# One step of a hybrid diffusion backbone: the scheduler's machine model is exchanged

## The chip, the cores and the metric

The kernel runs on one core of a Trainium2 chip. What is compared is the device time of one execution in microseconds. A core has five engines that each work through an instruction queue of their own, in the order in which the program holds it: TensorE (PE in the rows; its weight loads are PEld), VectorE (DVE), ScalarE (ACT), GpSimd (POOL) and SyncE (SP). Here SP does nothing but issue DMAs.

## What is computed

One layer on 512 latent and 128 context tokens of width 1024 (640 tokens together), cut to what matters:

```python
h = _rmsnorm(x, p['norm1_g']) * (1.0 + sc1) + sh1        # sc, sh, g from cond @ ada_w
u = h @ p['w_in']                                        # ONE input projection
y_a = _pool_mixer(z_pool, ...)                           # window means
y_b = _fourier_mixer(z_four)                             # 2-D Fourier per group
y_c = rwkv7(r, k, v, w, kk, a)                           # bidirectional, state 64x64
y_d = gla_chunked(q, kg, vg, log_a)                      # bidirectional, gated linear attention
branch = einsum('blic,icd->blid', stack(y_a, y_b, y_c, y_d), p['w_branch'])
gates = sigmoid(m_log)                                   # 4 x 1024 columns of u
out = sum(gates * branch, axis=2) @ p['w_out']
xf = x + g1 * out
h = _rmsnorm(xf, p['norm2_g']) * (1.0 + sc2) + sh2
xf = xf + g2 * (square(relu(h @ p['mlp_w1'])) @ p['mlp_w2'])
y = _rmsnorm(xf, final_g)
```

The outputs are the normalised tokens and the final RWKV and GLA states of the context.

## The kernel before

**Arithmetic.** Large products are made from two halves: an operand is split into a rounded part and a rest (`wh`/`wl`, `xh`/`xl`), and three products are added up in PSUM (`terms`, L363 to L369, for the first half of the kernel; `hidden`, L1356, and L1407 for the MLP). A weight tile comes by DMA into one of three buffers `wr` (`fetch`, L238), is rounded on ScalarE (L246) and its rest is formed on VectorE (L247); two pairs `wh`/`wl` exist.

**Units of work.** `proj(c0)` (L475) makes 128 columns of the input projection for all 640 tokens: 8 k-steps x 3 terms x 2 halves = 48 matmuls of line L368, into one of two PSUM pairs `pm`. There are 51 such tiles; 32 of them are gate columns, made by `gate(i, dt)` (L1187) for mixer i, which ends in a Tanh on ScalarE into one of three buffers `gate`. `branch(i, dt, y)` (L1194) projects a mixer's output with 12 matmuls of L368.

**Stages in the order of the source.** The head (L379 to L472) normalises the tokens and makes the first conditioning columns. Pool and Fourier mixers follow (L522 to L597), then the rest of the conditioning (`ada_rest`, L319: VectorE sums of line L309 over weights `araw`, closed by small matmuls at L315 or L335). The RWKV mixer (L686 to L980) runs twice, for two pairs of heads; each pass builds its triangular matrices (L775), inverts them on VectorE (a loop of 30 dependent steps, L798 to L803) and then takes 8 dependent steps over chunks (L915 to L965: matmuls L921, L935, L944 with VectorE and ScalarE copies between). The GLA mixer (L996 to L1176) has seven levels, each with VectorE and ScalarE work before five matmuls of L1084. The source then lists the merging (L1218 to L1233): for mixers 0 and 1 gate and branch per 128 columns; for mixer 2 the eight gates are made ahead and parked in DRAM (`gscr`, L1224) until the RWKV output is there. Mixer 3 is merged with the output projection (L1250 to L1274). The MLP (L1354 to L1440) is four groups of 8 hidden tiles (L1361, 48 matmuls of 320 columns each) and two halves of the down projection (L1407), the last half apart at L1427.

**What sets the order.** The source is not the order of execution. The framework traces all instructions with their dependencies, and when the `TileContext` closes, its scheduler lays them out: it plays the program on a model of the machine, and each time an engine is free in that model it hands it the instruction of the highest priority that is ready there, and gives out buffers as it goes. Priority follows the order of the source, except in `hi()` and `first()` blocks (L141 to L149), which are raised. So the projections and gates, which depend on nothing but `xh`, `xl` and their weights, are put wherever the model sees TensorE free while RWKV or GLA work isn't ready. The order that results is written into the five queues. The model's durations decide that order and nothing else.

The line that changes is in `kernel()`:

## Time and profile before

| | us |
|---|---|
| median of 3 runs | 1223.72 (1221.15 to 1225.99) |
| the profiled execution, its own time | 1224.66 |
| its span from first to last instruction | 1222.9 |
| TensorE busy / VectorE / ScalarE / GpSimd | 1176.4 / 733.5 / 506.7 / 62.3 |
| mean granted TensorE clock | 0.988 |

Busy time is the union of an engine's instructions. A matmul's end is modelled, so that a busy TensorE is not one at its peak; its true rate is read from the time that a run of equal matmuls takes. In tables of stretches the columns are from:to, the length, then busy us (and instructions) of PE, PEld, DVE, ACT and POOL, the granted clock as a share of full speed, the busy share of the DMA engines and GB/s. "Chain" is the chain of work that ended last, followed back from the last instruction through whatever released each step.

### The profile page before, as it was taken

The numbers are of one execution on the slowest core, as the hardware profiler recorded it, in microseconds if no ns is written. First come the engines' busy times: TensorE is split into PE (matmuls) and PEld (weight loads), VectorE is DVE, ScalarE is ACT, GpSimd is POOL, SyncE is SP. The second block draws the span as 40 slices with busy tenths as digits, with TensorE's granted clock in tenths as the row PEclk, the third lists the DMA queues.
The fourth block names the chain that finished last, engine by engine and source line by source line (L and its number), as shares of the span: only waits on it lengthen the run. The fifth ranks groups of instructions, "written<-read, shape, count | busy, mean of one in ns | idle before, by whom it ended". The sixth has DMA issues, their size and how long they took to land.

```text
span 1222.9 us, 19633 instructions
## 1 busy us (share of the span) xinstructions
PE 1176.4 (96%) x7556; PEld 1017.1 (83%) x7556; DVE 733.5 (60%) x1458; ACT 506.7 (41%) x1028; POOL 62.3 (5%) x98
## 2 busy tenths in 40 slices
PE   7999999899999999997999989999999999999996
PEld 2778998789778898795588978998899899889985
DVE  4797785675588583447987757543443354245456
ACT  4732225742376522378635325532143123213332
POOL 0000000500114200300000000000000000000000
PEclk9999898999999999999999999999999999999999
DMA  9558661334314343056624560322222222222222
GB/s 357 205 173 251 201 224 57 104 93 119 101 36 122 103 148 95 30 170 212 195 93 141 179 208 18 99 75 69 77 79 85 71 79 78 70 87 69 78 87 86
DMA packets 85971, 147.41 MB, mean 121 GB/s; under 512 B 21693, under 2 KB 26206, under 8 KB 85878
## 3 DMA queue, kind: packets, MB, share of 16 engines
q1 hardware_dynamic: 85878, 146.16, 37.8%
q8 instruction: 59, 0.97, 0.3%
q14 instruction: 34, 0.28, 0.1%
HBM read 123.17 MB, written 22.95 MB: 119 GB/s over the span
## 4 chain that ended last, share of the span: by engine, by line
PE 77%; DVE 8%; DMA 7%; ACT 4%; issue 3%; SPq 0%; POOL 0%; DVEq 0%; ACTq 0%; POOLq 0%
PE pt L368 23%; PE pf L1361 18%; PE pf L1407 16%; PE po L1247 3%; PE pf L1427 2%; PE px L1084 2%; DMA araw<-in_t_ada_dram 2%; PE px L499 2%; DVE acc L309 2%; DVE wl L247 1%; PE px L287 1%; DMA wr<-in_t_in_dram 1%; DMA wr<-in_t_out_dram 1%; DMA wr<-in_t_w_dram 1%; PE px L775 1%
## 5 line engine op out<-in xcount | busy, mean ns | idle before, releaser
L246 ACT CAST wh<-wr 128x512 fp32r<-128x512 f32 x222 | 133.4, 618 | 349.5 <-PE pf L1407 139.1
L247 DVE TENSOR_TENSOR wl<-wr,wh 128x512 fp32r<-128x512 f32 x222 | 152.2, 700 | 206.9 <-ACT wh L246 202.4
L368 PE MATMUL pt<-xl,wh 128*128 128x320 f32 x816 | 200.5, 321 | 0.0
L368 PE MATMUL pt<-xh,wh 128*128 128x320 f32 x816 | 199.7, 321 | 0.0
L368 PE MATMUL pt<-xh,wl 128*128 128x320 f32 x816 | 196.1, 318 | 0.0
L1361 PE MATMUL pf<-nh,wl 128*128 128x320 f32 x512 | 158.1, 309 | 0.0
L1361 PE MATMUL pf<-nl,wh 128*128 128x320 f32 x512 | 158.0, 309 | 0.0
L1361 PE MATMUL pf<-nh,wh 128*128 128x320 f32 x512 | 157.9, 309 | 0.0
L368 PEld LDWEIGHTS pt<-xh,wh 128*128 128x128 f32 x816 | 138.9, 191 | 8.8 <-issue 4.1
L368 PEld LDWEIGHTS pt<-xl,wh 128*128 128x128 f32 x816 | 139.5, 191 | 6.8 <-issue 3.0
L368 PEld LDWEIGHTS pt<-xh,wl 128*128 128x128 f32 x816 | 138.9, 191 | 4.9 <-issue 1.7
L1407 PE MATMUL pf<-wl,fh 128*128 128x512 f32 x280 | 109.0, 389 | 0.0
L1407 PE MATMUL pf<-wh,fh 128*128 128x512 f32 x280 | 109.0, 389 | 0.0
L1407 PE MATMUL pf<-wh,fl 128*128 128x512 f32 x280 | 108.9, 389 | 0.0
L1361 PEld LDWEIGHTS pf<-nl,wh 128*128 128x128 f32 x512 | 96.0, 187 | 0.2
L1361 PEld LDWEIGHTS pf<-nh,wh 128*128 128x128 f32 x512 | 96.0, 188 | 0.1
L1361 PEld LDWEIGHTS pf<-nh,wl 128*128 128x128 f32 x512 | 96.0, 187 | 0.0
L309 DVE SCALAR_TENSOR_TENSOR acc<-araw,sc,acc 128x512 f32<-128x512 f32 x112 | 78.4, 746 | 11.9 <-DMA araw<-in_t_ada_dram 11.9
L1407 PEld LDWEIGHTS pf<-wh,fl 128*128 128x128 f32 x280 | 52.6, 188 | 11.0
L1407 PEld LDWEIGHTS pf<-wh,fh 128*128 128x128 f32 x280 | 52.6, 188 | 10.9
L1407 PEld LDWEIGHTS pf<-wl,fh 128*128 128x128 f32 x280 | 52.6, 188 | 10.7
L1366 DVE TENSOR_TENSOR rl<-rl,pf 128x320 f32<-128x320 f32 x64 | 31.0, 484 | 39.0 <-ACT rl L1365 39.0
(540 smaller groups left out, 1754.2 us busy)
## 6 DMA issues: line engine op xcount, KB each, us to landing
wr<-in_t_w_dram SPq DMA_DIRECT2D x128, 256.0 KB, 3.0
wr<-in_t_in_dram SPq DMA_DIRECT2D x102, 256.0 KB, 3.5
araw<-in_t_ada_dram SPq DMA_DIRECT2D x64, 256.0 KB, 3.5
adaw<-in_t_ada_dram SPq DMA_DIRECT2D x16, 512.0 KB, 9.2
mscr<-gate SPq DMA_DIRECT2D x24, 320.0 KB, 4.3
mg<-mscr SPq DMA_DIRECT2D x24, 320.0 KB, 3.8
uscr<-mg SPq DMA_DIRECT2D x15, 320.0 KB, 2.8
wr<-in_t_branch_dram SPq DMA_DIRECT2D x32, 128.0 KB, 2.1
```

The source lines that it names most:

```text
L246: S.copy(wh, raw)
L247: V.tensor_tensor(wl, raw, f32(wh), ALU.subtract)
L287: PE.matmul(pt[0:8, :], lhsT=c[:, 4 * part : 4 * part + 8, k + j], rhs=w[:, j], start=part == 1 and k + j == 0 and n == 0, stop=part == 0 ...
L309: V.scalar_tensor_tensor(acc[j], raw, w, acc[j], ALU.mult, ALU.add)
L368: PE.matmul(pt[:, b, :HN], lhsT=w, rhs=m[:, b * HN : b * HN + HN], start=start and n == 0, stop=stop and n == 2)
L499: PE.matmul(pt[:, :HN], lhsT=lhsT, rhs=rhs[:, b * HN : b * HN + HN], start=True, stop=True)
L1084: PE.matmul(pt, lhsT=ek[:, ts_], rhs=em[:, :, ts_], start=True, stop=True)
L1247: PE.matmul(acc, lhsT=m[k][:, sl_], rhs=W[k, hf][w][:, 0, :], start=k == 0 and n == 0, stop=k == KT - 1 and n == 2)
L1361: PE.matmul(pt[:, :HN], lhsT=wk[:, k, :], rhs=m[:, k, bs], start=k == 0 and n == 0, stop=k == KT - 1 and n == 2)
L1366: V.tensor_tensor(rl, rl, pt[:, :HN], ALU.mult)
L1407: PE.matmul(acc[i], lhsT=m[k][:, ts_], rhs=w[:, kk, :], start=k == 0 and n == 0, stop=k == 7 and n == 2)
L1427: PE.matmul(acc, lhsT=m[k][:, ts_], rhs=ws[k][w][:, 0, :], start=k == 0 and n == 0, stop=k == 7 and n == 2)
```

## The change

The context is told to schedule on the framework's timeline model of the machine instead of its default model. No instruction of the source is added, removed or altered, and no priority, buffer count or pool changes. What can change is the order in each engine's queue, which buffer of a ring a tile gets, with that where waits stand, and the loads of activation tables on ScalarE, which are put in where the order needs another table.

```diff
-    with _tile.TileContext(nc) as tc:
+    with _tile.TileContext(nc, schedule_with_timeline_sim=True) as tc:
         backbone(tc, args, *outs)
```

## Rows read from the trace of the kernel before

**Rows 1.** The page's busy times: us, share of the span, instructions.

```profile
PE 1176.4 (96%) x7556; PEld 1017.1 (83%) x7556; DVE 733.5 (60%) x1458; ACT 506.7 (41%) x1028; POOL 62.3 (5%) x98
```

**Rows 2.** The page's chain that ended last, by engine.

```profile
PE 77%; DVE 8%; DMA 7%; ACT 4%; issue 3%; SPq 0%; POOL 0%; DVEq 0%; ACTq 0%; POOLq 0%
```

**Rows 3.** Stretches by stage, columns as told under time and profile.

```profile
0.00:7.70 7.70, 0.00 (x0) 0.00 (x0) 2.73 (x21) 1.59 (x3) 1.57 (x6) 1.00 0.72 204
7.70:211.00 203.30, 196.42 (x1100) 161.46 (x1100) 149.46 (x267) 84.14 (x145) 1.57 (x3) 0.96 0.63 213
211.00:367.00 156.00, 151.83 (x1358) 129.29 (x1357) 102.97 (x234) 81.08 (x182) 26.63 (x43) 1.00 0.31 89
367.00:513.00 146.00, 142.75 (x1318) 123.77 (x1319) 89.47 (x205) 60.29 (x150) 26.27 (x42) 1.00 0.35 104
513.00:541.00 28.00, 27.65 (x163) 24.27 (x162) 11.28 (x20) 16.49 (x24) 6.31 (x5) 1.00 0.42 135
541.00:667.00 126.00, 114.88 (x594) 87.17 (x593) 102.70 (x172) 79.05 (x142) 0.00 (x0) 0.97 0.49 156
667.00:774.20 107.20, 103.61 (x569) 90.71 (x568) 72.25 (x152) 46.30 (x102) 0.00 (x0) 1.00 0.44 142
774.20:1213.50 439.30, 439.28 (x2465) 400.43 (x2463) 198.79 (x380) 136.37 (x280) 0.00 (x0) 1.00 0.25 77
```

**Rows 4.** The chain in order of time: start us, us, what (count).

```profile
262.06 30.12 PE pt L368 x204
...
560.23 4.53 PE px L1084 x10
...
880.40 56.32 PE pf L1361 x384
```

**Rows 5.** The chain within the RWKV stretch, 211 to 513 us, by line.

```profile
by line: PE pt L368 54.4%; PE px L775 3.2%; PE px L499 3.1%; PE pxc L944 3.0%; PE pxc L935 2.6%; PE pxc L921 2.6%; issue 2.1%; PE px L823 2.1%; PE pxc L909 1.9%; PE pxc L905 1.5%; DVE wl L247 1.5%; DVE sl L741 1.3%; DMA ut<-uscr 1.2%; PE px
```

**Rows 6.** The chain within the GLA stretch, 541 to 667 us, by line.

```profile
by line: PE pt L368 23.6%; PE px L1084 19.4%; issue 7.0%; DMA wr<-in_t_in_dram 4.2%; ACT eqm L1080 3.7%; DMA mg<-mscr 3.7%; DMA gate<-gscr 3.6%; DMA gt<-uscr 2.7%; DVE att L1091 2.7%; DVE wl L247 2.4%; PE px L1153 2.0%; PE px L499 1.7%; ACT
```

**Rows 7.** Waits of TensorE: for whom, us in total, times, longest us.

```profile
PE pxa L315 <- DVE acc L309: 3.5, 3, 1.7
PE px L775 <- ACT sl L781: 3.4, 4, 1.7
PE px L775 <- DVE big L757: 2.1, 2, 1.6
...
PE pt L368 <- ACT bh L246: 2.0, 4, 1.3
...
PE pxa L335 <- DVE acc L309: 1.5, 1, 1.5
```

**Rows 8.** The four stretches before 700 us at half clock, columns as in Rows 3.

```profile
124.89:135.12 10.24, 10.24 (x43) 10.24 (x43) 5.07 (x12) 0.83 (x1) 0.00 (x0) 0.50 0.50 160
...
sum 23.89, PE 23.86 PEld 20.53 DVE 13.19 ACT 7.83 POOL 0.00; mean PE 5.96 PEld 5.13 DVE 3.30 ACT 1.96 POOL 0.00
```

**Rows 9.** TensorE in order of time around 122 us: start, us, what, [idle before].

```profile
124.53 0.38 PE L315 MATMUL pxa<-ones,acc 128*128 128x1 f32 x2 [1.68 <-DVE acc L309]
```

**Rows 10.** ScalarE in order of time around 520 us, columns as in Rows 9.

```profile
517.80 1.28 ACT L510 ACT_TABLE_LOAD   x1
...
519.65 1.28 ACT L1191 ACT_TABLE_LOAD   x1
520.94 0.70 ACT L1191 ACTIVATE gate<-pt 128x640 f32<-128x640 f32 x1
521.66 1.28 ACT L510 ACT_TABLE_LOAD   x1
...
523.51 1.28 ACT L512 ACT_TABLE_LOAD   x1
```

**Rows 11.** SP's own queue, its longest wait, columns as in Rows 7.

```profile
SPq L241 <- DVE wl L247: 496.7, 188, 20.6
```

**Rows 12.** One of the page's costliest groups: xcount | busy us, mean ns | idle before, releaser.

```profile
L247 DVE TENSOR_TENSOR wl<-wr,wh 128x512 fp32r<-128x512 f32 x222 | 152.2, 700 | 206.9 <-ACT wh L246 202.4
```

## Prediction

> **What bounds the kernel now.** I read the busy times first: TensorE is busy 96% of the span, VectorE 60% [rows 1]. Then the chain that ended last: 77% of it is TensorE [rows 2]. Those two say that TensorE bounds the kernel, but not where there is room, so the third view is the table by stage [rows 3]. Its last line is the MLP: from 774.2 to 1213.5 us TensorE is busy 439.28 of 439.30 us at full clock, and the chain there is one unbroken run of matmuls, 384 in 56.32 us, that is 146.7 ns each [rows 4]. With the 9.4 us of the last normalisation and stores behind it, some 449 us of the span are a wall: an order can only make them worse.
>
> All that another order can win lies before 774.2 us. TensorE's idle time there, from the same table, is 203.30 - 196.42 = 6.88, 4.17, 3.25, 0.35, 11.12 and 3.59 us in the six stretches from 7.7 us on, 29.4 us in sum; the first 7.7 us wait for the first constants under either order. To that comes a loss of clock: 23.89 us ran at half clock [rows 8], in which 11.9 us of full-clock work were done, so 11.9 us were lost. The first of these stretches begins at 124.89 us, 0.4 us after TensorE had stood still for 1.68 us ahead of a small matmul of the conditioning sums (L315) whose input VectorE hadn't finished [rows 9]. **The most that a perfect order could give is therefore 29.4 + 11.9 = 41.3 us, 3.4%.** The default model's order is already close to what the chip does; that is the first thing that the profile says about the change.
>
> The second thing is that the two long stages are of different kinds. In the RWKV stretch (211 to 513 us) the projections of line L368 are 54.4% of the chain [rows 5]: TensorE has work to fill every wait with, and the filling itself is what takes the time. In the GLA stretch (541 to 667 us) L368 is 23.6% [rows 6]; the rest are dependent steps, their matmuls, VectorE (busy 102.70 of 126 us), ScalarE and transfers, and TensorE idles 11.12 us [rows 3]. Projections are one stock that both stages draw on, and it matters which stage uses them.
>
> **The change part by part.** No instruction of the source is added or removed: the MLP's matmuls, those of L368 and all DMAs stay. So the first term is 0, and everything comes from order. The trace of before shows no row of the new order; each effect is bounded by the nearest rows.
>
> (a) Where projections go. One projection is 48 matmuls; 204 of them took 30.12 us [rows 4], 147.6 ns each, so a projection is 48 x 147.6 = 7.09 us of TensorE. A model that sees longer waits in the RWKV steps puts more of them ahead of a step's next matmul; a model that sees shorter ones puts fewer. On the chip a projection put ahead delays the RWKV step by 7.09 us, and the GLA stretch gives back only the part in which L368 was on its chain, 23.6%: the net price is 7.09 x 0.764 = 5.4 us. How many? At least 0. At most 8: the gates of mixer 2 can all go ahead, because they are parked in DRAM and wait for no branch. Below nothing too, if they are held back instead; that gain is bounded by the 11.12 us that TensorE idles in the GLA stretch. I take 2 in the direction of the loss, because two weight pairs and two PSUM pairs are what lets TensorE have two projections ready at a time, so that one misjudged wait admits two. That is 2 x 5.4 = 10.8 us; the ends are 8 x 5.4 = 43.3 us and -11.1 us. I choose the loss because in the RWKV stretch TensorE idles only 4.17 + 3.25 us of 302 [rows 3], so that a changed order has little to find there and much to spend.
>
> (b) Waits that TensorE now meets at the head of its queue. For the conditioning sums 3.5 + 1.5 us, for the RWKV matrices 3.4 + 2.1 us, for branch weights 2.0 us [rows 7], 12.5 us in sum; with the first half-clock stretch (10.24 us, 5.1 us lost [rows 8]) 17.6 us. A model that knows when these inputs come would put projections there. But each is a misjudged moment of one model, and another model misjudges others: between -17.6 and +17.6 us, and I take 0.
>
> (c) SP's queue. It holds 188 weight loads that wait for a buffer to be freed by VectorE, up to 20.6 us at a time [rows 11], and behind each such load stand the reads of parked gates, partial sums and GLA inputs. Moving one of those reads behind or ahead of a weight load shows where its transfer is on the chain: in the GLA stretch 3.7% of 126 us for the partial sums, 3.6% for the parked gates, 2.7% for the GLA inputs [rows 6], together 10.0% or 12.6 us. Both ends are 12.6 us either way; I take 0.
>
> (d) Activation tables. From 517.80 to 524.79 us four loads of 1.28 us stand close together, because one gate's Tanh falls between the two Ln of a normalisation and the Exp follows [rows 10]. With the gate elsewhere two of the four fall away, 2 x 1.28 = 2.6 us; an order that puts another gate there adds as much. I take 0, because in that stretch TensorE is busy 27.65 of 28 us [rows 3] and the projections hide ScalarE; without that cover it is 2.6 us on the chain. The Trainium skill, page "ScalarE: Activation LUTs", section "Table sets: the hidden batching unit", says that functions of one table set should be called together, and that Ln and Exp share a set, so that Ln and then Exp cost one load. Rows 10 differ: a load stands between them at 523.51 us. The same page puts a switch at about 2.66 us with its drain; the rows show 1.28 us and the next activation 0.01 us after its end. By the page's figure term (d) would be an estimated 5.3 us instead of 2.6 us; by both it is taken at 0 here.
>
> (e) The MLP. The order there follows from the data and the rings: 0. If a weight tile came late there its price stands below.
>
> Sum: 1224.66 (the profiled execution's own time: span 1222.9 and 1.8 us around it) + 10.8 = 1235.5, and since that execution lies 0.9 us above the median of the runs shown, 1235 us, +0.9%.
>
> **The rivals.** *Forecast, 41%:* projections run ahead of the RWKV steps and are missing in the GLA stretch: 1228 to 1268 us (1224.7 + 43.3), likeliest 1235. For it: the two shares of L368 on the chain. Against it: nothing in the trace tells the sign.
>
> *Faster, 31%:* the timeline model knows better when VectorE's sums and casts end, TensorE doesn't meet those waits, and the clock isn't lost behind them: -17.6 us, 1207 us; if the other half-clock stretches go too (11.9 - 5.1 = 6.8 us), 1200 us. For it: these waits are real, each with other ready work in the queue behind it. Against it: they are small, and there is no reason that no new ones arise. It decides from the point where it returns more than 10.8 us, about three fifths of its waits.
>
> *No change, 22%:* TensorE is full in both orders, projections fill whatever waits there are, gains and losses under (a) to (d) cancel: 1224 us, within 6 us. The case that the option doesn't alter the order at all falls here, with the same time.
>
> *The MLP is hurt, 6%:* raised loads and casts there are interleaved so that a hidden tile's second weight half is late by one cast's rest. The slack is wide (VectorE 198.79 and ScalarE 136.37 of 439.30 us [rows 3]), which speaks against it; if it happened at each of the 32 hidden tiles by one VectorE split, 700 ns [rows 12], it would cost 22 us: 1247 us.
>
> **How the numbers follow.** The predicted time is the forecast's, 1235 us. A measurement of this kernel can tell about 0.5% (6 us) from no change. Slower by more: forecast and MLP, 0.47. Faster: 0.31. Within: 0.22. The range goes from the fuller recovery of the faster rival, 1200 us, to eight projections ahead, 1268 us; about one in ten lies beyond each end. Between the signs this is nearly even; the forecast's own range is 1228 to 1268 us.
>
> **What would show it.** In the table by stage the stretch after 774 us should be as long as before, with TensorE's idle time there under 1 us. The first matmul of the GLA levels (L1084) should come later than at 560.23 us [rows 4], and fewer than the present L368 matmuls should lie between it and the last of them; TensorE's idle time in that stretch should grow beyond 11 us. I am wrong by sign if the GLA levels begin earlier or the waits for the conditioning sums and the half-clock stretch behind them are gone while nothing takes their place; wrong in the wall if the MLP's runs of L1361 take more than 56.3 us.

## The result and the profile after

The kernel after takes 1276.78 us (1276.64 to 1280.77) where the kernel before took 1224.86 us on the same chip: a ratio of 1.0435, interval 1.04 to 1.0469, 52 us slower. The forecast was 1235 us within 1200 to 1268. The sign was right, the size wrong by 42 us, and the range too short by 9. The prediction called the signs nearly even and said that nothing in the trace told them apart, so a good part of the right sign is luck.

The page of the kernel after: busy us of PE to POOL (share of the span) and instructions, the granted TensorE clock in 40 slices of the span, and the chain that ended last by engine.

```profile
PE 1197.7 (94%) x7556; PEld 1037.7 (81%) x7556; DVE 732.7 (57%) x1458; ACT 505.9 (40%) x1028; POOL 62.1 (5%) x98
...
PEclk9999999999999998556997999999999999999999
...
PE 70%; DVE 11%; DMA 10%; ACT 6%; issue 3%; SPq 1%; DVEq 0%; ACTq 0%
```

The work is the same, instruction for instruction (compare [rows 1]); TensorE's share of the chain fell from 77% to 70% [rows 2], and VectorE, ScalarE and transfers took what it lost. The clock row has a hole in the middle that the kernel before hasn't (its row first, then the stretch of the hole in the kernel after, at 0.50, the lower of the clock's two levels):

```profile
PEclk9999898999999999999999999999999999999999
```

```profile
505.10:590.43 85.33, 62.70 (x566) 47.42 (x562) 35.08 (x83) 30.16 (x68) 11.62 (x16) 0.50 0.21 66
```

Where that hole lies is seen in the table by stretch, cut here at the events that both kernels share: first group of RWKV step matmuls (L935) and last RWKV matmul (L909) of each pair of heads, first matmul of the GLA levels (L1084), first matmul of the output projection (L1247), start of the unbroken MLP. First before, then after:

```profile
305.70:354.40 48.70, 48.12 (x521) 36.70 (x518) 30.41 (x76) 22.76 (x55) 6.62 (x13) 1.00 0.21 64
354.40:471.10 116.70, 113.45 (x873) 102.18 (x867) 85.20 (x176) 60.55 (x133) 21.12 (x30) 1.00 0.42 124
471.10:512.20 41.10, 41.10 (x518) 31.71 (x519) 16.47 (x48) 10.93 (x38) 4.36 (x11) 1.00 0.16 45
512.20:560.20 48.00, 45.42 (x285) 40.94 (x282) 26.05 (x43) 33.61 (x52) 7.09 (x5) 1.00 0.51 166
560.20:664.90 104.70, 95.81 (x467) 69.28 (x467) 86.09 (x145) 61.35 (x114) 0.00 (x0) 0.97 0.46 144
664.90:774.00 109.10, 105.50 (x582) 92.46 (x581) 74.02 (x156) 47.00 (x103) 0.00 (x0) 1.00 0.44 144
```

```profile
295.80:404.60 108.80, 106.55 (x938) 93.98 (x939) 53.95 (x117) 38.18 (x86) 5.79 (x13) 0.98 0.37 111
404.60:506.90 102.30, 99.36 (x792) 89.46 (x788) 67.07 (x145) 53.47 (x116) 19.85 (x30) 0.99 0.36 109
506.90:548.90 42.00, 33.34 (x423) 27.04 (x418) 13.02 (x44) 7.26 (x32) 4.77 (x12) 0.50 0.01 3
548.90:596.50 47.60, 29.02 (x85) 19.82 (x81) 28.14 (x51) 28.25 (x45) 6.85 (x5) 0.54 0.40 128
596.50:707.10 110.60, 95.71 (x449) 71.50 (x450) 77.44 (x128) 58.73 (x106) 0.00 (x0) 0.89 0.37 116
707.10:829.80 122.70, 112.39 (x602) 96.25 (x600) 77.94 (x160) 51.53 (x115) 0.00 (x0) 0.98 0.39 129
```

And the matmuls of L368, the projections, alone: in the steps of the second pair and between RWKV and GLA, before and after.

```profile
471.10:512.20 41.10, 24.03 (x102) 15.30 (x101) 1.00 0.16 45
512.20:560.20 48.00, 39.10 (x247) 36.46 (x247) 1.00 0.51 166
```

```profile
295.80:404.60 108.80, 85.10 (x506) 75.91 (x505) 0.98 0.37 111
...
506.90:548.90 42.00, 0.00 (x0) 0.00 (x0) 0.50 0.01 3
548.90:596.50 47.60, 14.68 (x48) 11.62 (x48) 0.54 0.40 128
```

What to see: the steps of the first pair carry 505 projection matmuls where they carried 124, and last 108.8 us instead of 48.7. The steps of the second pair carry none where they carried 101, and are no shorter (42.0 against 41.1 us). The stretch from RWKV to GLA carries 48 where it carried 247, and is as long as before (47.6 against 48.0 us), with TensorE idle for 18.6 of them. RWKV ends 36.7 us later (548.9 against 512.2), with 213 more projection matmuls done; at the 147.6 ns of [rows 4] these are 31.4 us. Nothing of this is given back: 0.4 us between RWKV and GLA, then a further 5.9 us lost in the GLA stretch and 13.6 us in the output stage. 36.7 - 0.4 + 5.9 + 13.6 and 0.1 for the rest are the 55.9 us between the two spans.

The 36.7 us hide a gain of 9.9 us in the head, which ends at 295.8 instead of 305.7 us (part of it differs from one execution to the next, as told at the end). From the first L935 on, RWKV is 46.6 us longer with 199 more projection matmuls, which are 29.4 us at that price. Most of the 17 us that are left belong to the second pair's steps: their 101 (14.9 us) were moved out, and the steps got no shorter.

### The profile page after: what moved, and what is told of

Same layout as the page of the kernel before. It is cut to its first block, busy times and chain, and to the rows that moved or that the text cites. A ratio compares the mean times of both kernels' runs of the same rounds, so it can differ in the third digit from the quotient of the medians.

```text
span 1278.8 us, 19669 instructions
## 1 busy us (share of the span) xinstructions
PE 1197.7 (94%) x7556; PEld 1037.7 (81%) x7556; DVE 732.7 (57%) x1458; ACT 505.9 (40%) x1028; POOL 62.1 (5%) x98
## 4 chain that ended last, share of the span: by engine, by line
PE 70%; DVE 11%; DMA 10%; ACT 6%; issue 3%; SPq 1%; DVEq 0%; ACTq 0%
PE pt L368 22%; PE pf L1361 18%; PE pf L1407 15%; DMA araw<-in_t_ada_dram 3%; PE po L1247 3%; DVE acc L309 2%; PE pf L1427 2%; DMA wr<-in_t_out_dram 2%; PE px L499 1%; DMA wr<-in_t_in_dram 1%; DVE wl L247 1%; PE pxc L944 1%; PE px L775 1%; ACT eqm L1080 1%; DMA adaw<-in_t_ada_dram 1%
## 5 line engine op out<-in xcount | busy, mean ns | idle before, releaser
L247 DVE TENSOR_TENSOR wl<-wr,wh 128x512 fp32r<-128x512 f32 x222 | 146.3, 690 | 200.4 <-ACT wh L246 199.7
L246 ACT CAST wh<-wr 128x512 fp32r<-128x512 f32 x222 | 127.9, 618 | 309.8 <-PE pf L1407 119.8
L368 PE MATMUL pt<-xh,wh 128*128 128x320 f32 x816 | 198.3, 321 | 4.9 <-ACT gate L1191 2.5
L368 PE MATMUL pt<-xl,wh 128*128 128x320 f32 x816 | 196.5, 319 | 0.0
L368 PE MATMUL pt<-xh,wl 128*128 128x320 f32 x816 | 196.3, 319 | 0.0
L1361 PE MATMUL pf<-nh,wh 128*128 128x320 f32 x512 | 159.3, 311 | 2.7 <-ACT nh L1338 2.7
L1361 PE MATMUL pf<-nl,wh 128*128 128x320 f32 x512 | 159.3, 311 | 0.0
L1361 PE MATMUL pf<-nh,wl 128*128 128x320 f32 x512 | 159.1, 311 | 0.0
L368 PEld LDWEIGHTS pt<-xh,wh 128*128 128x128 f32 x816 | 138.8, 191 | 15.0 <-issue 4.6
L368 PEld LDWEIGHTS pt<-xl,wh 128*128 128x128 f32 x816 | 139.3, 191 | 7.2 <-issue 5.4
L368 PEld LDWEIGHTS pt<-xh,wl 128*128 128x128 f32 x816 | 139.0, 191 | 6.2 <-issue 4.3
L1407 PE MATMUL pf<-wh,fl 128*128 128x512 f32 x280 | 108.9, 389 | 0.0
L1361 PEld LDWEIGHTS pf<-nh,wh 128*128 128x128 f32 x512 | 97.0, 190 | 3.1 <-ACT nh L1338 3.0
L1361 PEld LDWEIGHTS pf<-nl,wh 128*128 128x128 f32 x512 | 97.1, 190 | 0.3 <-DVE nl L1339 0.2
L1361 PEld LDWEIGHTS pf<-nh,wl 128*128 128x128 f32 x512 | 97.1, 190 | 0.0
L309 DVE SCALAR_TENSOR_TENSOR acc<-araw,sc,acc 128x512 f32<-128x512 f32 x112 | 79.6, 743 | 10.2 <-DMA araw<-in_t_ada_dram 10.0
L1407 PEld LDWEIGHTS pf<-wh,fh 128*128 128x128 f32 x280 | 52.5, 188 | 10.8
L368 PE MATMUL pt<-yh,bh 128*128 128x320 f32 x128 | 35.8, 361 | 16.8 <-ACT yh L624 8.7
```

What stands on the lines that cost most here:

```text
L246: S.copy(wh, raw)
L247: V.tensor_tensor(wl, raw, f32(wh), ALU.subtract)
L309: V.scalar_tensor_tensor(acc[j], raw, w, acc[j], ALU.mult, ALU.add)
L368: PE.matmul(pt[:, b, :HN], lhsT=w, rhs=m[:, b * HN : b * HN + HN], start=start and n == 0, stop=stop and n == 2)
L1361: PE.matmul(pt[:, :HN], lhsT=wk[:, k, :], rhs=m[:, k, bs], start=k == 0 and n == 0, stop=k == KT - 1 and n == 2)
L1407: PE.matmul(acc[i], lhsT=m[k][:, ts_], rhs=w[:, kk, :], start=k == 0 and n == 0, stop=k == 7 and n == 2)
```

## The experiments

All lengths are read from the profiles at the same events. In the table each cell is a length in us and, in brackets, the projection matmuls in it; "to 1st" is the time of the first L935 (cells are cut at the events themselves and can differ by 0.1 us from the rows shown). "Bare" steps are those without a projection among them. The code is cut to the lines that matter. The kernel before took 1219 to 1225 us beside each of these runs.

| kernel | to 1st | first steps | between | second steps | RWKV to GLA | GLA | output |
|---|---|---|---|---|---|---|---|
| before | 305.7 | 48.7 (124) | 116.8 (563) | 41.1 (101) | 48.0 (247) | 104.7 (278) | 109.1 (264) |
| after | 295.8 | 108.9 (505) | 102.3 (482) | 41.9 (0) | 47.6 (48) | 110.6 (264) | 122.7 (264) |
| t_warm | 296.1 | 108.3 (505) | 103.0 (482) | 41.2 (0) | 46.2 (48) | 106.5 (264) | 125.3 (264) |
| t_hold5 | 296.3 | 106.6 (505) | 101.2 (290) | 61.0 (192) | 47.3 (48) | 108.5 (264) | 124.0 (264) |
| t_hold1h | 294.6 | 96.9 (402) | 115.8 (585) | 41.0 (0) | 47.4 (48) | 111.1 (264) | 123.9 (264) |
| t_hold1 | 295.5 | 70.9 (162) | 121.4 (621) | 60.6 (204) | 48.7 (48) | 108.1 (264) | 123.6 (264) |
| t_hold1p | 298.1 | 72.8 (162) | 121.4 (621) | 95.7 (496) | 53.5 (140) | 99.3 (72) | 96.0 (72) |
| t_park3 | 295.6 | 107.2 (505) | 116.5 (596) | 69.1 (270) | 47.3 (48) | 98.0 (72) | 95.5 (72) |
| t_fill4 | 297.1 | 106.3 (505) | 100.7 (290) | 48.1 (39) | 60.1 (213) | 102.1 (252) | 124.6 (264) |
| t_fill4h | 297.6 | 72.2 (162) | 121.4 (621) | 47.7 (51) | 60.1 (213) | 102.6 (252) | 124.2 (264) |
| d_push8 | 301.5 | 48.6 (124) | 156.7 (829) | 47.5 (48) | 59.1 (87) | 97.4 (225) | 106.8 (264) |
| d_push4 | 302.2 | 48.6 (124) | 135.9 (690) | 43.2 (114) | 62.8 (160) | 96.2 (225) | 109.4 (264) |
| d_park3 | 303.2 | 48.7 (124) | 116.8 (563) | 41.1 (101) | 54.6 (299) | 148.2 (418) | 120.0 (72) |
| d_peT | 315.1 | 116.0 (505) | 103.3 (482) | 41.6 (0) | 50.0 (48) | 112.6 (264) | 119.8 (264) |
| t_peD | 311.2 | 52.5 (124) | 124.2 (563) | 47.0 (101) | 62.2 (247) | 118.6 (278) | 119.8 (264) |
| d_peTD | 312.8 | 110.7 (505) | 103.4 (482) | 41.6 (0) | 45.7 (34) | 105.0 (278) | 107.1 (264) |
| d_peDT | 300.9 | 48.6 (124) | 117.1 (563) | 41.1 (101) | 76.8 (261) | 114.0 (264) | 119.1 (264) |
| d_block | 299.5 | 48.6 (124) | 116.8 (563) | 41.1 (101) | 73.3 (247) | 103.3 (278) | 107.2 (264) |
| d_bare | 301.3 | 48.6 (124) | 132.0 (664) | 38.0 (0) | 51.7 (247) | 105.8 (278) | 106.7 (264) |
| a_head | 296.2 | 48.7 (110) | 116.8 (563) | 41.1 (101) | 50.1 (247) | 105.7 (278) | 108.0 (264) |

### Is it the clock, or the bare steps?

**t_hold5** starts from the kernel after and fills its bare steps: five gates of mixer 2 are queued behind the first group of matmuls (L921, its last one kept in `marks`) of the second pair's steps 0 to 4.

```diff
-        g = gate(2, dt)
+        with (tc.issue_after(marks[1, dt - 3].ins) if dt > 2 else ExitStack()): g = gate(2, dt)
```

> The kernel after, in which the projections of five of mixer 2's eight parked gates are queued on TensorE behind the first matmul of steps 0 to 4 of the second RWKV pass; nothing else is changed. In the order after, all 2256 matmuls of L368 that don't hang on the RWKV output are used up before that pass takes its first step; held back, 240 of them lie within its steps and 2016 ahead of them. Stock theory (the loss comes from projections spent early): the second pass begins its steps some 25 to 35 us sooner (240 x 0.148 us = 35 us less ahead of it) and its steps have work to fill them, so the 85 us at half clock go away and the time falls by 25 to 40 us, to 1237 to 1252. Rival, the other waits of the new order (its output stage, its GLA stage and its buffers) carry the loss: 1270 to 1280, as the kernel after.

Measured 1295.61 us, ratio 1.0628 (1.0595 to 1.0661): slower, not faster. The filled steps grew from 41.9 to 61.0 us for 192 matmuls, and the inversion ahead of them, which had hidden 163, kept 48 and was no shorter (28.9 us against 27.5).

**t_warm** keeps TensorE's clock up in those steps with two extra matmuls of 256 columns ahead of each L935 and L944 group.

```diff
+            warm = lambda t: [PE.matmul(t[:, :256], lhsT=ident, rhs=cst[:, :256], start=True, stop=True) for _ in range(2 * hp)]
-            pu = pxc()
+            pu = pxc(); warm(pu)
-                pn = pxc()
+                pn = pxc(); warm(pn)
```

> The kernel after, with two extra matmuls of 256 columns ahead of the L935 and of the L944 matmuls of each step of the second RWKV pass, into the PSUM tile that those then overwrite; they only keep TensorE busy. Clock theory (the half clock in the bare stretch is a large part of the loss): the steps run at full clock, the three groups of small matmuls of a step take 2.1 us less, 8 steps 17 us less, and with the rest of the 85 us at half clock the time falls by 15 to 25 us, to 1252 to 1262. Stock theory alone (the clock is only a sign of it): within 6 us of 1277, or above it by the extra matmuls, at most 30 x 0.43 us = 13 us.

Measured 1274.99 us, ratio 1.0465 (1.0433 to 1.0497), as the kernel after. Its steps and the stretch behind them:

```profile
507.40:549.00 41.60, 36.62 (x474) 27.16 (x470) 13.95 (x44) 7.36 (x34) 4.68 (x12) 0.86 0.02 3
549.00:595.00 46.00, 26.93 (x79) 18.89 (x80) 27.68 (x50) 27.55 (x44) 6.68 (x5) 0.62 0.40 132
```

The granted clock rose from 0.50 to 0.86 and the steps stayed at 41 to 42 us. The extra matmuls (1.13 us a group) may have eaten what the clock gave, so this doesn't price the clock; the steps of d_bare, below, do. The second row holds no extra matmuls; its clock came up a little (0.54 to 0.62) and its length is nearly the same (46.0 against 47.6 us). The half clock goes with the loss; what part of it the clock makes in the steps is read there.

### Does moving projections ahead lose on the default model too?

**d_push8** is the kernel before with mixer 2's eight gates raised in priority; **d_push4** raises four.

```diff
-        g = gate(2, dt)
+        with tc.high_priority(offset=100000): g = gate(2, dt)
```

> The kernel before, on the default model, in which the projections of mixer 2's eight parked gates are raised above the RWKV steps in priority. In its order 2256 instead of 2043 matmuls of L368 come before the second RWKV pass ends, 213 more, all within that pass's steps. Stock theory: the pass ends 213 x 0.148 = 31 us later, the stretch from there to the first GLA level (48 us) doesn't shrink although its projections are gone, and the time rises by 25 to 31 us, to 1248 to 1255. By my prediction's price, with 23.6% returned, it would be 24 us. Rival (it is the timeline model's misjudged waits, not the stock): 1224, within 6 us.

> The kernel before with mixer 2's gates 0 to 3 alone raised in priority (half of the dose of the run with all eight): 140 more projection matmuls stand ahead of the end of RWKV, and 160 are left instead of 247 for the stretch from there to GLA. Theory: the 140 cost their full 0.148 us each ahead (20.7 us at the end of RWKV), the stretch to GLA stays at 47 to 50 us, and part of the 20.7 us comes back in the GLA stretch (53 matmuls fewer there, up to 7.8 us): 1230 to 1242 us. Rival, a threshold (only a bare stretch loses): 1216 to 1226 us.

d_push8: 1269.68 us, ratio 1.0424 (1.0386 to 1.0463). d_push4: 1247.91 us, ratio 1.0195 (1.0149 to 1.024). So the timeline model isn't needed for the loss: 213 projection matmuls more ahead of RWKV's end make it end 42.0 us later (554.2 against 512.2), 140 more 17.8 us later. Both expectations were too low, because the stretch to GLA didn't stay at 48 us with fewer of them; it grew to 59.1 us with 87 and to 62.8 us with 160. The number in a stretch was not the whole story; why just these two are so long wasn't followed to its end.

### First theory: the first pair's steps are over-filled

The steps of the first pair had grown by 60 us, so my first theory was that projections queued among them are the loss, and that held back behind them they would partly be hidden. **t_hold1** queues mixer 1's eight units behind the first group of matmuls of the first pair's last step, **t_hold1h** four of them. **t_park3** and **d_park3** park mixer 3's gates in DRAM like mixer 2's, on the kernel after and before, so that they can leave the output stage; **t_hold1p** holds all eight units and parks. Of the second edit one of three places is shown.

```diff
-            merged(i, dt, gate(i, dt), branch(i, dt, y))
+            with (tc.issue_after(marks[0, 7].ins) if 8 * i + dt >= 8 else ExitStack()): merged(i, dt, gate(i, dt), branch(i, dt, y))
```

```diff
-    for dt in range(KT):
-        g = gate(2, dt)
+    for i, dt in ((i, dt) for i in (2, 3) for dt in range(KT)):
+        g = gate(i, dt)
         with hi():
-            nc.sync.dma_start(out=gscr[dt], in_=g)
+            nc.sync.dma_start(out=(gscr if i == 2 else gscr3)[dt], in_=g)
```

> The kernel after, with the eight units of mixer 1 (gate and its share of the branches, which the timeline order lays among the RWKV steps of the first head pair) queued on TensorE behind the first matmul of that head pair's last step. In the order of the instructions 232 projection matmuls then stand in that stage instead of 575. Over-filled steps (my theory): the steps of the first head pair (first to last L935) shrink from 103.9 us to 50 to 65 us, the held projections run afterwards in front of the inversion of the second head pair, where part of them lies beside VectorE work; the RWKV stretch ends 15 to 40 us earlier than in the kernel after, and the time is 1235 to 1262 us, what is left above the kernel before being the output stage (+13.6 us) and the GLA stretch (+6.6 us). Rival, the projections are full-price wherever they stand: the steps shrink but the stage behind them grows by as much, and the time stays at 1270 to 1282 us. Rival, something else in the order of the steps (copies, transposes) makes them long: the steps stay above 85 us.

> The kernel after, with only the last four of mixer 1's eight units held behind the first matmul of the first head pair's last step (smaller dose of the same edit). Over-filled steps: about half of the effect of holding all eight, the steps of the first head pair (first to last L935) last 70 to 90 us, and the time is 1250 to 1270 us. Rival, full price wherever they stand: 1270 to 1282 us. Rival, a threshold (the steps are long as soon as any projection stands between them): steps above 95 us and time as in the kernel after.

> The kernel after, in which the eight gates of mixer 3 are made ahead and parked in DRAM like those of mixer 2, and read back in the output stage. That adds 384 matmuls of L368 (56.7 us) to the stock that doesn't hang on the RWKV output. In its order 337 of them lie within the steps of the second RWKV pass. Stock theory: they fill the bare steps and the stretch behind them, where TensorE idles some 70 us, so the time falls by 35 to 55 us, to 1222 to 1242, and the output stage shrinks by the five projections it loses (35 us) as far as its weight loads allow. Rival (other waits): the projections only move and the RWKV pass ends later by 337 x 0.148 = 50 us, 1265 to 1280.

> All eight units of mixer 1 held as in the kernel with this edit alone, and mixer 3's eight gates parked in DRAM as mixer 2's are, so that they no longer wait for the output stage. If the stretches after the RWKV stretch have waits of their own that hide part of the projections, the output stage (122.7 us with 264 projection matmuls in the kernel after) falls to 95 to 100 us and the RWKV and GLA stretches take up less than that: 1215 to 1245 us. If moved projections are paid in full wherever they go, it equals the kernel with mixer 1's units held, within 8 us.

> The kernel before (default model), with mixer 3's eight gates parked in DRAM as mixer 2's are. In the order of the instructions they leave the output stage (264 projection matmuls there) for the GLA stretch and the stretch ahead of it, which has waits. If those waits hide part of them: the output stage falls from 109 us to 75 to 90 us, the stretches ahead grow by less, and the time is 1205 to 1220 us. If projections are paid in full there: 1220 to 1230 us. If parking costs more than it gives (eight more stores and loads in the queues): 1230 to 1245 us.

The theory fell. t_hold1: 1278.67 us, ratio 1.0487 (1.0457 to 1.0517). t_hold1h: 1280.84 us, 1.0502 (1.0477 to 1.0528). The first steps did shrink, to 70.9 and 96.9 us, and the stretches behind them grew by as much: RWKV ends at 548.9, 548.4 and 548.5 us in the kernel after, t_hold1h and t_hold1. t_park3: 1279.86 us, 1.0503 (1.0471 to 1.0535), RWKV's end 39.6 us later and the GLA and output stretches 39.8 us shorter. t_hold1p: 1285.64 us, 1.0541 (1.0514 to 1.0567). d_park3: 1281.77 us, 1.0509 (1.0468 to 1.0549), above all three of its ranges: 311 projections stand in front of the first output matmul, and neither that stretch nor the one behind hides them.

What they show is a price. Projections in the second pair's steps, in orders that the timeline model made, one row each of t_park3 and of t_hold1p:

```profile
519.40:588.50 69.10, 44.16 (x271) 39.79 (x270) 0.93 0.35 119
```

```profile
492.30:588.00 95.70, 80.29 (x497) 73.04 (x496) 1.00 0.28 91
```

Against the bare 41.9 us, 270 cost 27.2 us and 496 cost 53.8 us, 0.101 and 0.108 us each of their 0.148 (t_hold5 and t_hold1: 0.099 and 0.092). In the kernel before 101 make the same steps no longer than the bare ones. So a projection has two prices in the same steps. The number alone doesn't make the difference: in t_fill4, below, 39, all behind the first group of the last step, make the steps 6.2 us longer (48.1 against 41.9 us), no less than their full price of 5.8 us. That leaves the place.

### Second theory: the stock is spent before the stretch to GLA

**t_fill4** queues mixer 2's gates 4 to 7 behind the first group of matmuls of the last RWKV step; **t_fill4h** holds mixer 1's units as well.

```diff
-        g = gate(2, dt)
+        with (tc.issue_after(marks[1, 7].ins) if dt >= 4 else ExitStack()): g = gate(2, dt)
```

> The kernel after, with mixer 2's gates 4 to 7 (192 projection matmuls) queued on TensorE behind the first matmul of the last RWKV step, so that 213 projection matmuls instead of 48 stand between the RWKV part and the first level of GLA; the steps of the first head pair keep theirs. Theory now (each stretch of waits hides projections up to a limit, and the timeline order has spent its stock before two of them): the stretch from the end of RWKV to GLA stays at 47 to 50 us with 165 more matmuls in it, 24 to 28 us of loss less; the inversion stretch of the second head pair gives up some 190 matmuls and loses part of that again. Time 1246 to 1266 us. Rival (projections cost their full price wherever they stand, what is lost behind RWKV is set by something else): the stretch grows by 24 us and the time stays at 1272 to 1285 us.

> The same, and mixer 1's eight units held behind the last step of the first head pair, which makes the counts of projection matmuls of the four stretches (steps of the first pair 232, of the second 168, RWKV to GLA 213) close to those of the kernel before. Theory: the inversion stretch of the second pair keeps its filling, so more of the gain is left: steps of the first head pair as in the kernel with mixer 1 held (they lose 12 us more than in the kernel after), steps of the second pair 12 us less lost, RWKV to GLA 26 to 28 us less lost: 1240 to 1256 us. Rival, it is not the counts but the order in detail: 1270 us or more.

t_fill4: 1288.36 us, ratio 1.0527 (1.0475 to 1.0579). t_fill4h: 1275.17 us, 1.0416 (1.0374 to 1.0457). Both missed; t_fill4h fell to its rival, that the order in detail decides and not the counts. The stretch took 165 more (24.4 us of TensorE) and grew by 12.5 us, so half of them were hidden; but the inversion of the second pair (t_fill4: 28.4 us with no projection) or the steps lost what had filled them. Moving whole groups by hand changes the number in a stretch, not where they stand in it.

### TensorE's order alone, exchanged between the kernels

Both kernels trace the same instructions, so the order of one can be imposed on the other: one no-wait dependency from each instruction to its predecessor in the list, on TensorE only. The model in use lays out the other queues anew around that order. **d_peT** is the kernel before with TensorE's order of the kernel after, **t_peD** the reverse. **d_peTD** and **d_peDT** (default model) splice the two orders at the last RWKV matmul.

```diff
-        backbone(tc, args, *outs)
+        backbone(tc, args, *outs); _pe_order(tc, nc)
+    ...                  # p: the wanted order, as places in the traced list
+    pe = [i for i in nc.cur_bb.bb.instructions if str(i.engine).endswith("PE")]
+    for a, b in zip(p, p[1:]):
+        tc.add_manual_dep(pe[b], pe[a].name, mybir.DependencyInfo(mybir.DependencyClass.NoSync, mybir.DependencyReason.DATA), reason="pe_order")
```

> The kernel before (default model for all engines), with one thing imposed: TensorE's queue has, instruction by instruction, the order that it has in the kernel after. Theory (the loss is TensorE's order: how the projections stand among the dependent matmuls): 1268 to 1285 us, with the stretch from RWKV's end to GLA at 46 to 50 us with 48 projection matmuls and the second head pair's steps bare. Rival (orders of VectorE, ScalarE and the DMA queues carry a large part, such as the late loads of the output stage): 1224 to 1262 us.

> The counterpart: the kernel after (timeline model for all engines), with TensorE's queue in the order of the kernel before. Theory: 1215 to 1232 us, as the kernel before. Rival (the other engines' orders): 1235 to 1280 us.

> The kernel before with a spliced order of TensorE's queue: the order of the kernel after up to the last RWKV matmul, and behind it the rest in the relative order of the kernel before. The projections used early are gone, so 34 are left for the stretch from RWKV's end to GLA. Theory by the stretches' losses (second pair's steps +16 us, RWKV to GLA +29 us, both bare because of what was spent before them): those stay, and what the kernel after lost behind (first output matmuls +7, start of the MLP +6, GLA +3) comes back: 1252 to 1268 us. Rival, the order behind RWKV's end is what loses: 1220 to 1240 us.

> The other splice: the order of the kernel before up to the last RWKV matmul, and behind it the rest in the relative order of the kernel after, with 261 projection matmuls in the stretch from RWKV's end to GLA. Theory: that stretch is filled and loses nothing; only the parts behind it lose (up to 16 us): 1226 to 1242 us. Rival, the order behind RWKV's end is what loses: 1255 us or more.

d_peT: 1304.28 us, ratio 1.0654 (1.0615 to 1.0694). t_peD: 1278.61 us, 1.0432 (1.039 to 1.0474). Neither did what I expected: each kernel's order of TensorE is slow with the queues that the other model lays around it. Those queues are neither kernel's: in d_peT's trace VectorE's order differs from that of the kernel before in 769 of 1458 places and from that of the kernel after in 603. In t_peD TensorE stood at the head of its queue for weight halves that the other engines made later (waits of TensorE from 200 to 700 us; the kernel before waits 0.9 and 2.0 us on these two):

```profile
PE pt L368 <- DVE bl L247: 11.6, 3, 6.8
PE pt L368 <- ACT bh L246: 6.3, 5, 2.3
```

So a schedule is a set of queues that fit together, and the loss can't be put down to TensorE's queue by itself. The splices still divide it. d_peTD, 1276.36 us (1.0388 to 1.0456), has both bare stretches (41.6 us with none, 45.7 us with 34) and from GLA on the lengths of the kernel before:

```profile
614.20:719.20 105.00, 95.61 (x469) 69.73 (x467) 82.90 (x141) 59.97 (x113) 0.00 (x0) 0.97 0.43 136
719.20:826.30 107.10, 104.75 (x582) 92.62 (x581) 74.24 (x156) 47.04 (x103) 0.00 (x0) 1.00 0.43 146
```

That is 212.1 us, against 213.8 before and 233.3 after; d_peDT, with the order of the kernel after there, takes 233.1 us. So the 19.5 us lost behind the start of GLA belong to the order behind RWKV's end and not to what was spent ahead of it. It isn't TensorE's queue alone that makes them: t_peD has the order of the kernel before there and takes 238.4 us. d_peTD nevertheless missed its time, since its RWKV ends 19.6 us later than in the kernel after: the misfit of queues again. d_peDT, 1266.5 us (1.0312 to 1.0394), missed its first range, for its rival's, at the point that taught most. Its stretch from RWKV to GLA holds 261 projections and takes 76.8 us; here is the stretch cut behind the 213 that the splice puts first (L368 alone):

```profile
507.70:539.30 31.60, 31.46 (x213) 31.24 (x213) 1.00 0.30 94
539.30:584.50 45.20, 12.89 (x49) 10.04 (x48) 0.63 0.55 179
```

213 in 31.6 us, the full price, and then the stretch itself at 45.2 us, as if nothing had been done.

### Third theory: the place among the dependent matmuls

**d_block** is the kernel before with only this changed on TensorE: the same 213 matmuls stand right behind the last RWKV matmul instead of among the dependent ones of that stretch, and no matmul crosses its ends. **d_bare** moves the 101 of the second pair's steps right ahead of the steps. The orders that were imposed, told as lists (the kernels hold them as packed numbers):

```diff
+S = [i for i in D[rwkv_end:first_L1084] if i in T[:rwkv_end_of_T]]          # 213, all L368
+d_block = D[:rwkv_end] + S + [i for i in D[rwkv_end:] if i not in S]
+S = [i for i in D[first_step_of_pair_2:rwkv_end] if line[i] == 368]           # 101
+d_bare = D[:first_step_of_pair_2] + S + [i for i in D[first_step_of_pair_2:] if i not in S]
```

(D and T are the orders of TensorE in the kernels before and after.) The other queues are laid out anew here too: in the traces VectorE's order differs from that of the kernel before in 132 places between 515 and 645 us in d_block, and in 38 between 476 and 502 us in d_bare, among them the weight splits of the moved projections.

> The kernel before with one thing moved in TensorE's queue: the 213 projection matmuls that it has between RWKV's end and GLA, and the kernel after has earlier, stand in one block right behind the last RWKV matmul, in front of the dependent matmuls of that stretch, instead of among them. The stretch has the same 247 projection matmuls and nothing else is moved across its ends. Theory (a projection is hidden only where it stands in a wait between dependent matmuls): the block costs its full 213 x 0.148 = 31.5 us, the stretch grows from 48.0 us to 74 to 80 us, and the time is 1246 to 1258 us. Rival (the number in the stretch decides): 48 to 54 us and 1218 to 1230 us.

> The kernel before with the 101 projection matmuls that stand among the RWKV steps of the second head pair moved in one block right ahead of them, so that the steps are bare as in the kernel after. Theory: the bare steps last as long as the filled ones, 39 to 40 us, and the block costs its full 14.9 us: 1233 to 1243 us. Rival (a projection costs its time among the steps too): the steps fall to 24 to 30 us and the time stays at 1219 to 1228 us.

d_block: 1244.5 us, ratio 1.0199 (1.0169 to 1.023). L368 alone in the block, behind it, and in both:

```profile
506.10:537.70 31.60, 31.49 (x213) 31.24 (x213) 1.00 0.29 94
537.70:579.40 41.70, 8.83 (x35) 7.32 (x34) 0.67 0.42 140
506.10:579.40 73.30, 40.31 (x247) 38.56 (x247) 0.81 0.36 120
```

The same 247 projections take 73.3 us where they took 48.0: 25.3 us for the place alone (the block's 31.6 us, less 6.3 us because the rest, now nearly bare, takes 41.7). The time is 23.6 us above the kernel before on this chip, a little under my range. The chain behind the block shows what the projections had covered (chain in order of time: start us, us, what):

```profile
506.28 31.44 PE pt L368 x213
...
549.64 4.94 DMA gt<-uscr
...
566.84 5.95 DMA gt<-uscr
```

d_bare: 1233.22 us, ratio 1.0111 (1.0072 to 1.0151), in the range. L368 ahead of the steps and in them:

```profile
466.90:481.90 15.00, 15.00 (x102) 14.78 (x102) 1.00 0.33 102
481.90:519.90 38.00, 0.05 (x1) 0.00 (x0) 0.65 0.03 9
```

The bare steps take 38.0 us against 41.1 us with 101 projections among them. In the steps these 101 cost 3.1 us, ahead of them 15.0 us.

d_bare also prices the clock. Its bare steps ran partly at full clock (0.65 in the mean, 38.0 us), those of the kernel after at half clock (0.50, 42.0 us). Here are single steps of the second pair, from one L921 to the next, with the same dependent work: two of d_bare, then one each of the kernel after, of t_warm and of the kernel before (this last one with 11 projections).

```profile
499.36:502.86 3.50, 2.29 (x44) 1.72 (x41) 1.55 (x7) 1.11 (x7) 0.96 (x3) 1.00 0.00 0
507.24:511.52 4.28, 3.42 (x42) 2.76 (x41) 1.72 (x7) 0.59 (x3) 0.88 (x2) 0.50 0.01 4
```

```profile
536.24:540.52 4.28, 3.42 (x43) 2.76 (x41) 1.72 (x7) 0.59 (x3) 0.88 (x2) 0.50 0.02 4
```

```profile
536.77:541.07 4.30, 3.94 (x48) 2.87 (x49) 2.03 (x7) 0.59 (x4) 0.80 (x3) 1.00 0.00 0
```

```profile
499.97:504.41 4.44, 4.44 (x52) 3.36 (x51) 3.42 (x9) 2.39 (x6) 0.79 (x3) 1.00 0.41 132
```

A bare step takes 3.50 us at full and 4.28 us at half clock. So the half clock does cost the bare steps of the kernel after something: 0.78 us in each such step, and 4.0 us between the two sets of eight. In t_warm the extra matmuls took up what the clock gave back. The rows also say what makes the filling so cheap: 11 projections are 1.62 us at full price, and cost 0.94 us against a bare step at full clock, but only 0.16 us against the bare step at half clock that one gets without them.

**a_head** splices whole schedules, every engine's and queue's order imposed: that of the kernel after up to the first L935, then that of the kernel before.

> A splice of the two schedules with every engine's and queue's order imposed: all instructions that the timeline model schedules ahead of the first group of RWKV step matmuls (where the kernel after was 9.9 us ahead, 295.8 against 305.7 us, with 14 more projection matmuls done), then the rest in the order of the kernel before. If that head is worth its time by itself: 1207 to 1217 us, faster than both kernels. If the seam leaves engines waiting for what the other order would have prepared by then: 1220 to 1240 us.

Measured 1216.21 us, ratio 0.9967 (0.9942 to 0.9991), in its first range: faster than both kernels, by 0.3% of the kernel before. The head of the timeline model is a little better (first L935 at 296.2 us; the kernels with the other head reach it at 299.5 to 305.7 us with 14 fewer projections done), and with all queues spliced together the seam costs nothing that shows.

## Why the prediction was right or wrong

**What bounds the kernel: right.** The MLP is as long in both (449.0 us from its start to the end of the span; 384 matmuls of L1361 take 56.32 us in both, [rows 4]). All of the 55.9 us lie ahead of it. The default order was close to what the chip does: no run gained more than the 4.7 us of a_head.

**Term (a), the projections: the right place, under a third of the size.** The forecast's mechanism happened: RWKV was delayed by projections put ahead of it. The term said 10.8 us and the end of RWKV came 36.7 us later. Three steps in it were wrong.
- *How many.* I took 2 units of 48; 213 matmuls are 4.4. The reason that I gave, two weight and two PSUM pairs, bounds how many are ready at a time, but not how often the scheduler finds TensorE free in its model. At full price they are 31.4 us.
- *What comes back.* I took back 23.6%, the share of L368 on the chain of the GLA stretch [rows 6]. Nothing came back: the stretch from RWKV to GLA went from 48.0 to 47.6 us with 199 fewer. d_block and d_peDT show why. In the kernel before 213 of the 247 stood in waits of that stretch, where they cost 6.3 us (48.0 us against the 41.7 us without them in d_block), and in one block in front 31.6 us. A share of the chain is no price. I took it from 541 to 667 us, but it fails in the stretch itself: there L368 is 70.3% of the chain of the kernel before, and with 199 fewer the stretch is 0.4 us shorter, because the chain of copies, table loads and transfers beside it lasts nearly as long.

```profile
by line: PE pt L368 70.3%; DMA gate<-gscr 9.5%; PE pxc L499 8.2%; PE px L499 5.0%; issue 2.6%; DVE gate L1209 1.7%; ACT gate L1191 1.5%; PE pxc L909 0.8%; SPq L1224 0.7%
```

- *What I left out.* A step that loses its filling isn't shorter for it. The second pair's steps hid 101 projections for 3.1 us (d_bare); in the kernel after these stand elsewhere, and the steps are bare. I had read the RWKV stretch as "filled", from TensorE's idle time [rows 3, 5], and drew from it that the filling takes the time. In the steps it takes little, 3.1 us for 101, as long as it comes a few matmuls at a time.

The upper end, 8 units at 5.4 us, fell short for the price alone: at 7.09 us without the give-back it is 56.7 us, or 1281 us, and the range would have held the result.

The chain of the kernel after shows the bad place: steps of the first pair, in order of time (start us, us, what). 23 projections stand between L909 and L921, and 16 and then 2 more between L921 and L935, and within these 14 us L368 is 66.4% of the chain. What counts there is not the share but the lumps: the 381 projections that these steps have more than before cost 60.1 us, 0.158 us each, no less than their full price.

```profile
by line: PE pt L368 66.4%; PE px L499 18.2%; PE pxc L909 4.4%; PE pxc L905 3.4%; PE pxc L921 2.7%; PE pxc L935 2.7%; PE pxc L944 2.6%
...
339.97 0.61 PE pxc L909 x16
340.58 3.57 PE pt L368 x23
344.15 1.08 PE px L499 x4
345.23 0.38 PE pxc L921 x8
345.61 2.54 PE pt L368 x16
...
350.11 0.38 PE pxc L935 x8
```

**Term (b), waits at the head of the queue: taken at 0.** The half-clock stretch of 10.24 us at 124.89 us [rows 8] isn't there in the kernel after; two of 3.4 us, at 54.5 and 139.9 us, are. a_head measures what the whole order ahead of the first L935 is worth: 4.7 us, where I had 17.6 us as an end for these waits. Which of them carried it wasn't taken apart. It is the part of the faster rival that came true.

**Term (c), SP's queue: not confirmed.** 19.5 us were lost from GLA's start on, about a third of the whole, and the sum had nothing for them; the splices put them in the order behind RWKV's end. Whether SP's queue carries them, as its end of 12.6 us would have it, or VectorE's and ScalarE's late weight halves and splits (TensorE waits 5.2 us for a branch weight and 7.9 us for a split of the GLA output there), wasn't taken apart and stays open.

**Term (d), activation tables: no more loads, but not for the reason given.** Both executions have 17 table loads. I took 0 because projections hide them; behind RWKV that cover is gone, and in the kernel after two loads of 1.28 us (L512 at 557.50 and L1028 at 573.29 us) are on the chain of that stretch.

**Term (e) and the rivals.** The MLP was not hurt. "No change" failed because TensorE's being full [rows 3] didn't make its order indifferent.

**What was to show it.** L1084 came later, 596.5 instead of 560.23 us, and TensorE idled more (18.6 us from RWKV to GLA, where it had been 2.6, and 14.9 us in the GLA stretch as cut above, where it had been 8.9), as told. That fewer projections would lie between the first and the last L1084 was wrong: 118 instead of 92. They were missing ahead of GLA, not in it.

The Trainium skill, page "Perfetto Trace Analysis", section "Optimization Strategy", advises to interleave regimes that are bound by different engines. Here the trace agrees, and gives the size: 247 projections interleaved with the chain from RWKV to GLA take 48.0 us, and 73.3 us with 213 of them in front of it. The same skill's page "TensorE: Matmul & The Clock Gate", section "HAM oscillation — how this bites in real kernels", would have no long idle gaps of TensorE so that its clock stays up. The trace agrees that the clock is worth something even in these small steps (3.50 against 4.28 us), but matmuls put in for the clock alone, as in t_warm, took the gain up again (4.30 us). It differs on the gaps: in the second pair's steps of the kernel after TensorE never idles longer than 1.1 us at a time, and the clock is at half throughout; short gaps among small matmuls went with it here.

## What to carry to other kernels

Independent work was nearly free here only where it stood in waits between dependent instructions, a few instructions at a time; the same work in one block in front of them cost its full time, and the chain behind it gave little back. The share of such work on the chain (70.3% in the stretch from RWKV to GLA) doesn't tell the two apart. So before pricing a new order, count the filling in each dependent stretch, and ask for each what the stretch would last bare: here 38 to 42 us against 41.1 us with 101 projections, and 42 to 48 us with 34 or 48 against 48 us with 247. And take a scheduler's output as a set of queues: imposing the whole order of TensorE from one schedule on the other, with the rest laid out around it, lost 55 to 81 us here, while splicing whole schedules at one point kept the better part of each.

## What the runs showed of the hardware

- A dependent chain of small matmuls and copies does pay for the lower of the clock's two levels (1.2 GHz, granted 0.50), though far less than twofold: the same bare step took 3.50 us at 1.00 and 4.28 us at 0.50 (d_bare). Two extra matmuls ahead of each of two groups a step kept the clock at 1.00 and the step at 4.30 us (t_warm).
- In the nearly bare stretch behind its block, d_block took 41.7 us at a granted clock of 0.67; d_peTD, whose TensorE had come out of bare steps at half clock, took 45.7 us at 0.51 with the same 65 matmuls in the same order. The difference lies at the start: the first three groups of L499 were done 5.4 us behind the end of the block, with matmuls of 0.43 us, and 10.2 us behind the end of RWKV in d_peTD, with 0.74 us. Part of it is the clock, part the copies that ran under the block; how much of each wasn't tried.
- Two executions of one order can differ by some 6 us in the head: with the head of the kernel before, the same on every queue, the first L935 came between 299.5 and 305.7 us. The 9.9 us by which the kernel after's profile is ahead there are thus partly of this kind; a_head's 4.7 us is the measured value.
